# Attention products with the values issued directly behind the next step's transposes, instead of ahead of the transposes of the step after that

## Chip, cores and metric

The kernel runs on one core of a Trainium2 chip. The metric is the device time of one execution in microseconds (us), as the median of several runs. The core has a matrix engine (TensorE, PE in the profile; PEld is its weight load), a vector engine (DVE), an activation engine (ACT), GpSimd (POOL) and a queue that issues DMAs (SP). Each engine works through its own instructions in program order and waits at semaphores for the others.

## What is computed

One layer of a hybrid attention trunk for 1024 prompt frames and 64 sample frames, model width 1024. Two branches of 8 heads of 64 each: "sb" (stick-breaking attention over all earlier keys) and "cb" (softmax attention over a band of 640 keys with a relative bias). All is in float32. The part that the change touches is the attention itself:

```python
z = jnp.einsum("bqhd,bkhd->bhqk", q, k).astype(jnp.float32) * ATTN_SCALE
...
w = jnp.where(causal, jnp.exp(log_beta + suffix), 0.0)          # sb
return jnp.einsum("bhqk,bkhd->bqhd", w.astype(v.dtype), v)
...
p = jax.nn.softmax(s, axis=-1).astype(v.dtype)                  # cb
return jnp.einsum("...hqk,...khd->...qhd", p, v)
```

Before it stands one large input projection, and behind it the two gated branch projections and the output projection.

## The kernel before

The kernel is one program with an order written out by hand: each engine's instructions stand in the order in which the Python code emits them. About the first 547 us are the normalisation and the input projection (`L467`, `L673`). From 547 us to about 826 us the attention runs, and the last 145 us are the merge and the output projection (`L990`, `L1507`).

**The attention loop.** It goes through `seq`, a list of 136 steps: for each branch (sb, then cb) 4 pairs of heads, and for each pair 17 steps: one for the sample frames (t = 8, both heads at once), then 8 blocks of 128 prompt rows, each for head 0 and head 1. A step has four stages, which different iterations i of the loop issue:

- `qk(i)`, line 1096: the scores, PE matmuls in `F32R` of up to 512 columns into a PSUM tile `z` (three buffers; a step with more than 512 keys takes two). They are emptied by ACT for sb (the sigmoid of line 1099) and by DVE for cb (line 1101, `kp`/`sm` being its running minimum).
- `soft` and `mid`, in the next iteration or two: for sb one DVE scan over the row (line 1118), for cb an exponential on ACT (1109), a reciprocal on DVE (1120) and a scaling on ACT (1121).
- `tr(i - 4)`, line 1149: the weights `be`, 128 rows by up to 1024 keys, are transposed by PE, one 128 by 128 block an instruction, in groups of up to four into a PSUM tile `pt` (two buffers). Each group is copied out into `wT` by ACT (1158; 1154 for a block of 64 keys) or, three times in four in the cb branch, by DVE (1160). `LAG = 4` is the distance in steps.
- `av(b, p, j)`, line 1188: the product of transposed weights and values. One call serves 256 query rows, both heads: block pair j = 0 to 3, or j = 4 for the sample frames, so five calls for each pair of heads. The two heads use two halves of the PE array (64 columns each, `128*64` in the profile), while all other matmuls around use the whole array (`128*128`). The result stands in the PSUM tile `o` (one buffer); DVE multiplies it with the gate in `zt` (line 1197 in sb, 1199 in cb), and a POOL DMA stores it to `d_osb` or `d_ocb` (line 746, issued by `flush` an iteration later).

**Fills.** Matmuls of other projections are strewn between (`fill(n)`, lines 842 and 948, `acc`): one to three for a step in cb, fewer in sb. Half of an iteration's number stands ahead of the transposes, half behind.

**The queue of products.** When `tr` of the last step that a product needs has been issued, in iteration i, `avq` takes a note of it (line 1299), with the iteration i + 2 as its due time. The loop looks for due products (line 1293) just ahead of `tr`.

Of the kernel before, what the change touches and what calls it, by code (L numbers as in the profile page):

```python
# [32 lines left out]
def hybrid_step_kernel(ctx: ExitStack, tc: tile.TileContext, x_prompt, x_sample, c_sbk, c_sbv, c_cbk, c_cbv,  # L33
# [702 lines left out]
    def flush(every=False):  # L736
        todo = deferred[:]
        deferred.clear()
        for n, f in todo:
            if n <= 0 or every:  # L740
                f()
            else:
                deferred.append((n - 1, f))

    def store_later(dst, src, n=0):
        deferred.append((0, lambda: G.dma_start(dst, src)))  # L746
# [304 lines left out]
    def fill(n):  # L1051
        n += owed[0]
        owed[0] = 0
        while n > 0:
# [9 lines left out]
    seq = [(b, p, t, hd) for b in ("sb", "cb") for p in range(NPAIR) for t in [8] + list(range(8))  # L1064
           for hd in range(2) if t < 8 or hd == 0]

    def band(b, t):
        if t == 8:
            return 0, 576
        if b == "sb":  # L1070
            return 0, (t + 1) * 128
        k0 = max(0, t - 4)
        return k0, (t + 1 - k0) * 128
# [31 lines left out]
    def soft(i):  # L1105
        n = band(*seq[i][::2])[1]
        be, kp = st[i]
        j = 1 if n > 512 else 0
        A.activation(be[:, :n], be[:, :n], AF.Exp, bias=kp[:, j:j + 1], scale=-1.0, accum_out=kp[:, 2:3])  # L1109

    def mid(i):
        b, p, t, hd = seq[i]
        r = 128
        k0, n = band(b, t)
        be, kp = st[i]
        if b == "sb":
            im = ims[:] if t == 8 else imp[:, NP - n:NP]
            V.tensor_tensor_scan(be[:r, n - 1::-1], be[:r, n - 1::-1], im[:, ::-1], 0.0, op0=OP.mult, op1=OP.max)  # L1118
        else:
            V.reciprocal(kp[:r, 3:4], kp[:r, 2:3])  # L1120
            A.activation(be[:r, :n], be[:r, :n], AF.Copy, scale=kp[:r, 3:4])  # L1121

    def wbase(b, j):
        return max(0, 2 * j - 4) if b == "cb" and j < 4 else 0
# [3 lines left out]
    def tr(i):  # L1128
        b, p, t, hd = seq[i]
        r = 128  # L1130
        k0, n = band(b, t)
        be, _ = st.pop(i)
        j = t // 2 if t < 8 else 4
        q0 = (t % 2) * 128 if t < 8 else 0
        s0 = k0 - wbase(b, j)
        nblk = (n + 127) // 128
        groups = {}
        for kb in range(nblk):
            groups.setdefault((s0 + kb) // 4, []).append(kb)
        for g, kbs in groups.items():  # L1140
            wk = (b, p, j, hd, g)
            if wk not in wT:
                wT[wk] = ak.tile([128, 4, 256], F32, name="wT", bufs=6)
            w = wT[wk]
            pt = psT.tile([128, 4, 128], F32, name="pt")
            kr = 128
            for x, kb in enumerate(kbs):
                kr = min(128, n - kb * 128)
                TE.transpose(pt[:kr, x, :r], be[:r, kb * 128:kb * 128 + kr], ident[:r, :r])  # L1149
            m = len(kbs)  # L1150
            sl = (s0 + kbs[0]) % 4
            if kr < 128:
                m -= 1
                A.activation(w[:kr, sl + m, q0:q0 + r], pt[:kr, m, :r], AF.Copy)
            if m:
                flip[0] += 1
                if b == "sb" or flip[0] % 4 == 0:
                    A.activation(w[:, sl:sl + m, q0:q0 + r], pt[:, :m, :r], AF.Copy)  # L1158
                else:
                    V.tensor_copy(w[:, sl:sl + m, q0:q0 + r], pt[:, :m, :r])  # L1160


    def load_z(b, p, j):
        zt = ak.tile([128, 256], F32, name="zt", bufs=4)
        nq = 256 if j < 4 else 64
        SP.dma_start(zt[:, :nq], d_z[b][p][:, 256 * j:256 * j + nq])
        zts[b, p, j] = zt

    def av(b, p, j):
        o = psO.tile([128, 256], F32, name="o")  # L1170
        vp, vs = VP[b, p]
        if j == 4:
            nq = 64
            steps = [(kb, 0, 64) for kb in range(5)]
        else:
            nq = 256
            lo = 2 * j - 3 if b == "cb" else 0
            steps = [(kb, 0, 256) for kb in range(max(0, lo), 2 * j + 1)]
            if lo > 0:
                steps.append((lo - 1, 0, 128))  # L1180
            steps.append((2 * j + 1, 128, 256))
        base = wbase(b, j)
        for si, (kb, c0, c1) in enumerate(steps):
            vv = vp if j < 4 else vs
            kr = 64 if j == 4 and kb == 4 else 128
            s = kb - base
            for hd in range(2):
                TE.matmul(o[hd * 64:hd * 64 + 64, c0:c1], vv[:kr, kb, hd * 64:hd * 64 + 64],  # L1188
                          wT[b, p, j, hd, s // 4][:kr, s % 4, c0:c1] if j < 4 else
                          wT[b, p, j, 0, s // 4][:kr, s % 4, 64 * hd:64 * hd + 64],  # L1190
                          start=si == 0, stop=si == len(steps) - 1)
        os = zts.pop((b, p, j))
        if b == "sb":
            for x in range(0, nq, 128):
                y = min(x + 128, nq)
                c = 2 * j + x // 128
                V.scalar_tensor_tensor(os[:, x:y], o[:, x:y], vl[:, p, c:c + 1], os[:, x:y], op0=OP.add, op1=OP.mult)  # L1197
        else:
            V.tensor_tensor(out=os[:, :nq], in0=o[:, :nq], in1=os[:, :nq], op=OP.mult)
        o0 = 256 * (j % 3)  # L1200
        store_later(d_o[b][p][j // 3][:, o0:o0 + nq], os[:, :nq], 1)
        for k in [k for k in wT if k[:3] == (b, p, j)]:
            wT.pop(k)
# [22 lines left out]
    def load_bias(h):  # L1226
        bt = ab.tile([128, 640], F32, name="bias", bufs=4)
        src = d_rb[h][0:1, 127:128]
        SP.dma_start(bt, bass.AP(tensor=src.tensor, offset=src.offset, ap=[[767, 128], [1, 640]]))
        G.memset(bt[0:64, 576:640], BIG)  # L1230
        G.memset(bt[64:128, 0:64], BIG)
        BI[h] = bt
        if h % 2:
            bs = BI["s", h // 2] = ab.tile([128, 576], F32, name="bsm", bufs=1)
            for w in range(2):
                src = d_rb[h - 1 + w][0:1, 127:128]
                SP.dma_start(bs[64 * w:64 * w + 64], bass.AP(tensor=src.tensor, offset=src.offset,
                                                             ap=[[767, 64], [1, 576]]))
# [19 lines left out]
    LAG = 4  # L1258
    avq = []
    for i in range(len(seq) + LAG + 2):  # L1260
        m = 0
        if i < len(seq):
            b, p, t, hd = seq[i]
            if b == "cb" and p == 0 and t == 8 and hd == 0:
                sbx.close()
                yst = ExitStack()
                late["y"] = yst.enter_context(tc.tile_pool(name="ay", bufs=2))
            if (b, p, t, hd) == ("sb", 3, 6, 0):
                load_bias(0)
                load_bias(1)  # L1270
        if 0 < i <= len(seq) and seq[i - 1][0] == "cb":
            soft(i - 1)
        if 1 < i <= len(seq) + 1 and seq[i - 2][0] == "cb":
            mid(i - 2)
        if i < len(seq):
            qk(i)
            if hd == 0:
                if t % 2 == 1 or t == 8 and (b, p) != ("sb", 0):
                    load_z(b, p, t // 2 if t < 8 else 4)
                prefetch(b, p, t)  # L1280
            acc += amount[b] * wt[b](band(b, t)[1]) / tot[b]
            acc += early.get((b, p, t, hd), 0)
            m = int(acc) - emitted
            emitted += m
        else:
            m = 8
        if 0 < i <= len(seq) and seq[i - 1][0] == "sb":
            mid(i - 1)
        flush()
        if i == len(seq) // 2 + LAG + 3:  # L1290
            late["sb"] = True
        fill(m // 2)
        while avq and avq[0][0] <= i:
            av(*avq.pop(0)[1:])
        if 0 <= i - LAG < len(seq):
            tr(i - LAG)
            b, p, t, hd = seq[i - LAG]
            if t == 8 or hd == 1 and t % 2 == 1:
                avq.append((i + 2, b, p, t // 2 if t < 8 else 4))
        fill(m - m // 2)  # L1300
    flush(True)
    yst.close()
# [177 lines left out]
    for i in range(2):  # L1480
# [3 lines left out]
        for q, s in enumerate(OP_):  # L1484
# [14 lines left out]
            for c in range(2) if s != "b" else ():  # L1499
# [9 lines left out]
                p = ps[:]  # L1509
# [15 lines left out]
                if s in (3, 4, 5, 6):  # L1525
# [4 lines left out]
                    if s == 4:  # L1530
                        p, x = u3[c], xrs.pop((i, 1, 1, c))
# [61 lines left out]
```

## Time and profile before

| | us |
|---|---|
| runs of the kernel | 974.56 median of 3 (973.98 to 976.94) |
| the profiled execution, its own time | 972.79 |
| its span | 971.0 |
| of it up to the attention | 547 |
| attention | 279 |
| merge and output projection | 145 |

The profile is one execution. Its page gives busy times, the chain of work that ended last, and groups of instructions by line; other views used below are the waits (who waited for whom), the timeline (instructions in order of time, neighbours of one kind merged) and the windows (busy time of each engine in a stretch of time). In a timeline row the first number is the start, the second the length from the first start to the last end, in us. Matmuls overlap in PE's pipeline: the distance between two starts is the time that the first one costs, its own length is longer.

The TensorE clock was granted in full over the whole span after the first slice. In the attention DVE and ACT are busy most of the time too:

```profile
547.00:680.00 133.00, 130.91 (x1051) 106.85 (x1049) 102.19 (x129) 93.49 (x233) 15.77 (x32) 1.00 0.81 216
680.00:826.00 146.00, 143.12 (x1103) 125.47 (x1104) 103.61 (x373) 107.11 (x235) 31.90 (x48) 1.00 0.71 199
```

These are two windows, the sb and the cb part. The columns are: stretch, its length, then busy time and number of instructions of PE, PEld, DVE, ACT and POOL, the granted clock, the busy share of the DMA engines and GB/s.

### The profile page before, as it was taken

What the parts mean: (1) busy time and instruction counts of PE and PEld (TensorE: products, weight loads), DVE (VectorE), ACT (ScalarE), POOL (GpSimd) and SP (SyncE); (2) the same over time, 40 slices, a digit from 0 to 9 for tenths busy, and PEclk for the clock granted to TensorE, in tenths of its full rate; (3) what the DMA queues carried; (4) which work ended last, traced back from release to release, by engine and by line L of the source; (5) the groups of instructions that cost most, each with busy time, mean ns of one, the idle gap of its engine ahead of it and who ended that gap; (6) DMA issues with size and microseconds to landing.
All of it is one profiled execution on the core that took longest, in us unless ns stands there. A gap on an engine that the chain in (4) does not pass through costs nothing.

```text
span 971.0 us, 20418 instructions
## 1 busy us (share of the span) xinstructions
PE 951.1 (98%) x7604; PEld 906.3 (93%) x7604; DVE 590.2 (61%) x1166; ACT 477.4 (49%) x1056; POOL 394.5 (41%) x391
## 2 busy tenths in 40 slices
PE   5999999999999999999999999999999999999998
PEld 5999999999999999999999987787888888999998
DVE  5456665696454555543332298777678775499735
ACT  6544443344444343333332377668687775466220
POOL 3276664215454566655542200101520111586632
PEclk9999999999999999999999999999999999999999
DMA  7727567534646655555533997668699852862732
GB/s 237 224 88 246 197 219 251 182 93 133 182 139 192 183 179 175 156 177 171 165 90 101 279 252 196 186 175 241 207 278 263 226 144 75 254 203 70 222 118 92
DMA packets 173512, 176.28 MB, mean 182 GB/s; under 512 B 30753, under 2 KB 157597, under 8 KB 173286
## 3 DMA queue, kind: packets, MB, share of 16 engines
q1 hardware_dynamic: 161878, 159.98, 55.5%
q10 hardware_dynamic: 8720, 8.33, 2.7%
q0 software_dynamic: 2816, 6.69, 2.1%
q8 instruction: 60, 0.98, 0.5%
q14 instruction: 38, 0.31, 0.1%
HBM read 112.94 MB, written 62.00 MB: 180 GB/s over the span
## 4 chain that ended last, share of the span: by engine, by line
PE 92%; DMA 3%; ACT 2%; issue 1%; POOL 1%; DVE 1%; SPq 0%; ACTq 0%; POOLq 0%; DVEq 0%
PE b L673 30%; PE acc L467 20%; PE b L1507 8%; PE o L1188 7%; PE pt L1149 7%; PE z L1096 6%; PE b L990 5%; PE acc L948 4%; PE acc L842 2%; PE pk L352 1%; DMA wrawx<-in_w_in_dram 1%; DMA wraw<-in_w_in_dram 1%; DMA d_gcb<-sg 1%; PE pt L280 1%; ACT be L1109 1%
## 5 line engine op out<-in xcount | busy, mean ns | idle before, releaser
L1149 PE MATMUL pt<-ident,be 128*128 128x128 f32 (+1 forms) x568 | 87.5, 278 | 2.8 <-ACT wT L1158 1.9
L1096 PE MATMUL z<-ks,sq 128*128 128x320 f32 (+5 forms) x384 | 87.4, 336 | 1.7 <-DVE sm L1101 1.7
L1118 DVE TENSOR_TENSOR_SCAN be<-be,imp 128x128 f32<-128x128 f32 (+7 forms) x64 | 83.4, 1343 | 9.2 <-ACT be L1099 9.2
L1149 PEld LDWEIGHTS pt<-ident,be 128*128 128x128 f32 (+1 forms) x568 | 66.2, 140 | 16.2 <-issue 5.4
L1158 ACT ACTIVATE wT<-pt 128x512 f32<-128x512 f32 (+3 forms) x125 | 58.0, 496 | 41.7 <-PE pt L1149 41.2
L467 PE MATMUL acc<-whi,xa 128*128 128x256 f32 x256 | 74.2, 292 | 0.0
L467 PE MATMUL acc<-wlox,xm 128*128 128x256 f32 x256 | 70.8, 278 | 0.0
L467 PE MATMUL acc<-whi,xm 128*128 128x256 f32 x256 | 70.8, 278 | 0.0
L467 PE MATMUL acc<-wlo,xa 128*128 128x256 f32 x256 | 70.7, 278 | 0.0
L467 PE MATMUL acc<-whix,xb 128*128 128x256 f32 x256 | 70.6, 278 | 0.0
L467 PE MATMUL acc<-whix,xm 128*128 128x256 f32 x256 | 70.6, 278 | 0.0
L681 DVE TENSOR_TENSOR u<-b,s 128x256 f32<-128x256 f32 (+1 forms) x56 | 24.3, 440 | 73.5 <-PE b L673 72.4
L1096 PEld LDWEIGHTS z<-ks,sq 128*128 128x128 f32 x384 | 63.8, 190 | 3.4 <-DVE sm L1101 2.0
L1188 PE MATMUL o<-wT,vp 128*64 128x256 f32 (+1 forms) x608 | 64.2, 356 | 0.0
L1188 PEld LDWEIGHTS o<-wT,vp 128*64 128x64 f32 x608 | 40.3, 136 | 23.1 <-issue 6.2
L124 POOL TENSOR_TENSOR wlo<-wraw,whi 128x1024 fp32r<-128x1024 f32 x15 | 36.5, 2431 | 56.1 <-ACT whi L117 50.7
L1121 ACT ACTIVATE be<-be,sm 128x640 f32<-128x640 f32 (+5 forms) x68 | 47.5, 698 | 15.2 <-DVE sm L1120 14.8
L746 POOL DMA_DIRECT2D d_osb<-zt x20 | 10.8, 542 | 102.5 <-DVE zt L1197 63.9
L1099 ACT ACTIVATE be<-z 128x384 f32<-128x384 f32 (+6 forms) x104 | 47.8, 512 | 4.8 <-PE z L1096 4.1
L437 POOL TENSOR_TENSOR whix<-ws,whix 128x512 fp32r<-128x512 f32 x28 | 37.1, 1324 | 32.0 <-ACT whix L436 32.0
L1109 ACT ACTIVATE be<-be,sm 128x640 f32<-128x640 f32 (+5 forms) x68 | 47.5, 699 | 3.1 <-DVE sm L1101 2.5
L467 PEld LDWEIGHTS acc<-whi,xa 128*128 128x128 f32 x256 | 47.9, 188 | 0.1
(306 smaller groups left out, 3187.8 us busy)
## 6 DMA issues: line engine op xcount, KB each, us to landing
wraw<-in_w_in_dram SPq DMA_DIRECT2D x31, 512.0 KB, 4.5
wrawx<-in_w_in_dram SPq DMA_DIRECT2D x17, 512.0 KB, 4.2
sq<-d_qsbT SPq DMA_DIRECT2D x32, 192.0 KB, 4.8
sq<-d_qcbT SPq DMA_DIRECT2D x32, 192.0 KB, 5.2
xt<-in_x_prompt_dram SPq DMA_DIRECT2D x8, 512.0 KB, 5.4
d_kcbT<-hl SPq DMA_DIRECT2D x8, 512.0 KB, 4.3
d_qcbT<-hl SPq DMA_DIRECT2D x8, 512.0 KB, 3.1
d_ksbT<-hl SPq DMA_DIRECT2D x16, 256.0 KB, 2.9
```

The source lines that it names most:

```text
L467: TE.matmul(ps, x, w, start=m == 0, stop=m == len(steps) - 1)
L673: TE.matmul(ps[:, :m], w[:, hl_, k], right[s](x)[:, k, a:b], start=s < 3 and k == 0 and e == 0, stop=k == 3 and e == 2, skip_group_check=s ...
L990: TE.matmul(pp[uu][:, :n], w[:, p, uu * 128:uu * 128 + 128], g[:, a:e], start=p == 0 and m == 0, stop=p == NPAIR - 1 and m == 2)
L1096: TE.matmul(z[:, :m], s[:, e, q0:q0 + 128], ks[:, h, o + x:o + y], start=(e, h) == parts[0], stop=(e, h) == parts[-1])
L1099: A.activation(be[:r, x:y], z[:r, :m], AF.Sigmoid, scale=-0.125)
L1109: A.activation(be[:, :n], be[:, :n], AF.Exp, bias=kp[:, j:j + 1], scale=-1.0, accum_out=kp[:, 2:3])
L1118: V.tensor_tensor_scan(be[:r, n - 1::-1], be[:r, n - 1::-1], im[:, ::-1], 0.0, op0=OP.mult, op1=OP.max)
L1121: A.activation(be[:r, :n], be[:r, :n], AF.Copy, scale=kp[:r, 3:4])
L1149: TE.transpose(pt[:kr, x, :r], be[:r, kb * 128:kb * 128 + kr], ident[:r, :r])
L1158: A.activation(w[:, sl:sl + m, q0:q0 + r], pt[:, :m, :r], AF.Copy)
L1188: TE.matmul(o[hd * 64:hd * 64 + 64, c0:c1], vv[:kr, kb, hd * 64:hd * 64 + 64], wT[b, p, j, hd, s // 4][:kr, s % 4, c0:c1] if j < 4 else wT ...
L1507: TE.matmul(ps[:, t], left[s](xs_, k)[:, ts_], wt_[:, k], start=s < 3 and t == k == e == 0, stop=k == 3 and e == 2, skip_group_check=s > 2 ...
```

## The change

A product is no longer due two iterations after its last transposes, ahead of that iteration's transposes. It is issued in the next iteration, directly behind that iteration's transposes and ahead of the second half of its fills.

```diff
         fill(m // 2)
-        while avq and avq[0][0] <= i:
-            av(*avq.pop(0)[1:])
         if 0 <= i - LAG < len(seq):
             tr(i - LAG)
+        for todo in avq:
+            av(*todo)
+        avq.clear()
+        if 0 <= i - LAG < len(seq):
             b, p, t, hd = seq[i - LAG]
             if t == 8 or hd == 1 and t % 2 == 1:
-                avq.append((i + 2, b, p, t // 2 if t < 8 else 4))
+                avq.append((b, p, t // 2 if t < 8 else 4))
         fill(m - m // 2)
```

So each of the 40 products moves, in program order, ahead of the second half of one iteration's fills, one `qk`, and the first half of the next iteration's fills. It stays between the same two groups of transposes.

On PE in the sb part, where there is no fill at this place: `o` is the product, `z` the scores, `pt` the transposes.

```order
 L1149 MATMUL pt<-ident,be 128x128 x5
-L1096 MATMUL z<-ks,sq_7420 128x448 x4
 L1188 MATMUL o<-wT,vp 64x256 x6
 L1188 MATMUL o<-wT,vp 64x128 x2
+L1096 MATMUL z<-ks,sq_7420 128x448 x4
 L1149 MATMUL pt<-ident,be 128x128 x5
```

The scores of the following step have gone from ahead of the product to behind it. What stood directly behind the product were transposes, and is now a score matmul.

On PE in the cb part, at the end of a pair of heads, where `acc` are the fills:

```order
 L1149 MATMUL pt<-ident,be 128x128 x5
-L948 MATMUL acc<-xa,whi 128x384
-L948 MATMUL acc<-xb,whi 128x384
-L1096 MATMUL z<-ks,sq_10015 128x128 x2
-L948 MATMUL acc<-xa,wlo 128x384
 L1188 MATMUL o<-wT,vp 64x256 x8
 L1188 MATMUL o<-wT,vp 64x128 x4
+L948 MATMUL acc<-xa,whi 128x384
+L948 MATMUL acc<-xb,whi 128x384
+L1096 MATMUL z<-ks,sq_10015 128x128 x2
+L948 MATMUL acc<-xa,wlo 128x384
 L1149 MATMUL pt<-ident,be 128x128 x5
```

Three fills and the scores have changed sides. The product is entered from transposes now, and left into a fill.

On DVE at such a place in the cb part, first before, then with the change. `zt` is the multiplication that empties the product, `be,sm` empties the scores, `wT` are copies of transposes:

```order
L1120 RECIPROCAL sm<-sm 128x1
L1101 ISA be,sm<-z,bias 128x128
L1101 ISA sm 128x1
L1199 TENSOR_TENSOR zt<-o,zt 128x256
L1160 COPY wT<-pt 128x4x128
L1160 COPY wT<-pt 128x128
```

```order
L1160 COPY wT<-pt 128x4x128
L1199 TENSOR_TENSOR zt<-o,zt 128x256
L1120 RECIPROCAL sm<-sm 128x1
L1101 ISA be,sm<-z,bias 128x128
L1101 ISA sm 128x1
L1160 COPY wT<-pt 128x4x128
L1160 COPY wT<-pt 128x128
```

The multiplication has moved from directly ahead of the copies of one group of transposes to ahead of the reciprocal and the emptying of the scores. On ACT and SP nothing changes its order; on POOL a few stores of products change places with a split of a weight block (line 124) or of a gated output (line 909).

## The prediction

> **What bounds the kernel now.** I read the page first, then the waits of PE within the attention (547 to 826 us), then PE's timeline at single products, and last DVE's and ACT's rows there.
>
> ```profile
> PE 951.1 (98%) x7604; PEld 906.3 (93%) x7604; DVE 590.2 (61%) x1166; ACT 477.4 (49%) x1056; POOL 394.5 (41%) x391
> PE 92%; DMA 3%; ACT 2%; issue 1%; POOL 1%; DVE 1%; SPq 0%; ACTq 0%; POOLq 0%; DVEq 0%
> ```
>
> PE is busy for 98% of the span, and 92% of the chain that ended last is PE's. So the time is the sum of PE's work and the change can act in two ways only: by what PE pays at the seams between kinds of matmuls, and by waits that it makes or removes. The waits in the attention are few:
>
> ```profile
> PE pt L1149 <- ACT wT L1158: 1.9, 5, 0.6
> PE z L1096 <- DVE sm L1101: 1.7, 1, 1.7
> PE pt L1149 <- DVE wT L1160: 0.7, 2, 0.4
> PE o L1188 <- PE z L1096: 0.3, 2, 0.2
> ```
>
> Columns: us in total, times, longest. In all 4.6 us of 279: that is the most that better order alone could take away. No product waits for its copies in `wT`, though it is the product that would be drawn nearer to them.
>
> **The change part by part.** It adds and removes no instruction. It moves 40 products, one for each store:
>
> ```profile
> L746 POOL DMA_DIRECT2D d_ocb<-zt x20 | 10.9, 547 | 72.2 <-DVE zt L1199 39.4 <-DVE sm L1120 17.7 <-DMA gt<-d_gsb 8.5
> L746 POOL DMA_DIRECT2D d_osb<-zt x20 | 10.8, 542 | 102.5 <-DVE zt L1197 63.9 <-DVE be L1118 16.2 <-DVE sm L1120 8.1
> ```
>
> First the seams. Products use half the array's columns for each head, all else the whole array. Two places show what entering and leaving a product costs. The last product of all stands between fills, the only such place before:
>
> ```profile
> 821.87 0.34 PE L948 MATMUL acc<-xa,wlo 128*128 128x384 f32 x1
> 822.04 0.34 PE L948 MATMUL acc<-xa,whi 128*128 128x384 f32 x1
> 822.31 2.38 PE L1188 MATMUL o<-wT,vp 128*64 128x256 f32 x24
> 824.62 0.44 PE L948 MATMUL acc<-xb,whi 128*128 128x384 f32 x1
> 824.90 0.33 PE L948 MATMUL acc<-xa,wlo 128*128 128x384 f32 x1
> 825.08 0.34 PE L948 MATMUL acc<-xa,whi 128*128 128x384 f32 x1
> ```
>
> A fill of 384 columns costs 0.17 to 0.18 us from start to start. The one ahead of the product costs 0.27: **entering** is 0.10. From the product's start to the next matmul's are 2.31 us. The first fill behind it is 0.44 long where others are 0.34, and the next starts 0.28 later instead of 0.17: **leaving into a fill** adds 0.105. Now the usual place, a product of the same 24 matmuls left into a transpose, and five transposes behind a product and not behind one:
>
> ```profile
> 753.80 2.38 PE L1188 MATMUL o<-wT,vp 128*64 128x256 f32 x24
> 756.11 0.33 PE L1149 MATMUL pt<-ident,be 128*128 128x128 f32 x1
> ...
> 815.59 0.76 PE L1149 MATMUL pt<-ident,be 128*128 128x128 f32 x5
> 816.11 0.42 PE L948 MATMUL acc<-xa,wlo 128*128 128x384 f32 x1
> 816.37 0.30 PE L948 MATMUL acc<-xa,whi 128*128 128x320 f32 x1
> ...
> 817.24 0.31 PE L948 MATMUL acc<-xa,whi 128*128 128x320 f32 x1
> 817.39 0.71 PE L1149 MATMUL pt<-ident,be 128*128 128x128 f32 x5
> 817.86 0.40 PE L948 MATMUL acc<-xb,whi 128*128 128x320 f32 x1
> 818.09 0.31 PE L948 MATMUL acc<-xa,wlo 128*128 128x320 f32 x1
> ```
>
> The product again takes 2.31. **Leaving into transposes** adds 0.05 (0.52 against 0.47 for five). A fill goes into transposes at no charge (0.15 for 320 columns, as between fills). A fill behind transposes shows 0.26 instead of 0.175 because it starts early, in the transposes' tail: five transposes truly cost 0.47 + 0.085 = 0.555.
>
> The last row of this kind needed, transposes into a product, is in no trace of before. Nearest are transposes that use 64 of the array's rows and are followed by a whole-array transpose or a fill:
>
> ```profile
> 59.47 0.34 PE L352 MATMUL pk<-ident,qn 64*128 64x64 f32 x2
> 59.73 0.66 PE L374 MATMUL pc<-ident,ck 128*128 128x128 f32 x4
> ...
> 87.14 0.34 PE L352 MATMUL pk<-ident,qn 64*128 64x64 f32 x2
> 87.40 0.39 PE L467 MATMUL acc<-whi,xa 128*128 128x256 f32 x1
> 87.63 0.28 PE L467 MATMUL acc<-whi,xm 128*128 128x256 f32 x1
> 87.75 0.28 PE L467 MATMUL acc<-wlo,xa 128*128 128x256 f32 x1
> ```
>
> Two transposes of 64 columns need half of two of 128, 2 x 0.055 = 0.11, and the second half of the price of leaving them: from 59.47 to 59.73 are 0.26, 0.15 over it. Of that 0.05 is what the first transpose behind a changed array costs (as above), so 0.10 is the emptying of the array, as much as a fill pays. It is the same whether a transpose or a fill follows (87.14 to 87.40). I therefore take 0.10 for transposes into a product. The last two rows give the price of leaving into a fill again: 0.23 against 0.12.
>
> The sum for one product, over the same matmuls, in starts (fill F, product P, five transposes T): before, F to P 0.27, P 2.31, T 0.52, F 0.26, together 3.36. After, F to T 0.175, T to P 0.555 + 0.10, P 2.31, F 0.28, together 3.42. That is **0.06 us more for each product**, all of it because the first matmul behind a product is now a fill or a score matmul (both load 128 columns in `F32R`) and waits longer for its weights than a transpose did. 40 x 0.06 = **+2.4 us**; with rounding of rows to 0.01 it may be 1.6 to 2.8, and I use +2.2. Bounds where the row is lacking: if T to P is free, 40 x (0.06 - 0.10) = -1.6; if it also pays 0.05 for the first weights, 40 x 0.11 = +4.4.
>
> The profile's two weight loads say where the 0.05 comes from:
>
> ```profile
> L1149 PEld LDWEIGHTS pt<-ident,be 128*128 128x128 f32 (+1 forms) x568 | 66.2, 140 | 16.2 <-issue 5.4
> L1096 PEld LDWEIGHTS z<-ks,sq 128*128 128x128 f32 x384 | 63.8, 190 | 3.4 <-DVE sm L1101 2.0
> ```
>
> A transpose's load lasts 140 ns, a score matmul's 190, a difference of 0.05. The Trainium skill says otherwise: by "TensorE: Matmul & The Clock Gate", section "LDWEIGHTS (loading the stationary operand)", a load depends on the number of columns alone, here 128 for both. By it leaving would cost the same either way, and the seams would sum to zero instead of +2.2. The rows speak against it, and I go by them.
>
> Next the waits. A product now stands only one step behind its last transposes. What hides the copies into `wT` is that iteration's scores, fills and transposes; with two groups the next transposes need the same `pt` buffers and so wait for these copies already. The tightest place is the first product of an sb pair, with single groups:
>
> ```profile
> 621.19 0.40 ACT L1158 ACTIVATE wT<-pt 128x256 f32<-128x256 f32 x1
> 621.24 0.49 PE L1149 MATMUL pt<-ident,be 128*128 128x128 f32 x3
> 621.45 0.80 ACT L1099 ACTIVATE be<-z 128x320 f32<-128x320 f32 x2
> ```
>
> The copy (first row) ends at 621.59, the three transposes' work at about 621.24 + 0.33 = 621.57: no wait, but no room. Were it 0.2 late at the 4 places, it cost 0.8. On DVE, the queue behind the multiplication of `zt` waits for the product's end, before as after; what is queued there changes from copies of transposes to a reciprocal and the emptying of the scores that now follow the product. At the ends of cb pairs this helps:
>
> ```profile
> 748.62 0.42 DVE L1199 TENSOR_TENSOR zt<-o,zt 128x256 f32<-128x256 f32 x1 [1.70 <-PE o L1188]
> 749.20 0.89 DVE L1160 COPY wT<-pt 128x512 f32<-128x512 f32 x2 [0.15 <-PE pt L1149]
> 749.94 0.77 PE L1149 MATMUL pt<-ident,be 128*128 128x128 f32 x5 [0.33 <-DVE wT L1160]
> ```
>
> Here copies queue behind the multiplication, and the next transposes wait. With the change the multiplication is done earlier: perhaps 0.3 at three places, -0.9. Against it, the scores' emptying in the middle of cb pairs, formerly done under the product, follows it now. I set the waits at zero, between -4.6 (all that there are) and what the first rival below costs. The one large wait, 1.69 us at 694.62, is a score matmul behind DVE, and the product that stood behind it moves ahead of it:
>
> ```profile
> 694.62 0.56 PE L1096 MATMUL z<-ks,sq 128*128 128x320 f32 x2 [1.69 <-DVE sm L1101]
> 695.40 0.87 PE L1188 MATMUL o<-wT,vp 128*64 128x256 f32 x8
> ```
>
> It can hide up to 0.87 of that wait, but DVE, late there, makes the following scores wait instead: zero again. Stores are issued one iteration earlier in the same queue; a weight split on POOL that now stands behind one more store is many fills ahead of its use. SP's order stays.
>
> Sum: 972.79 + 2.2 = 975.0 for an execution like the profiled one, which lay 1.8 under the median of its kernel's runs. In terms of that median: 974.56 + 2.2 = **976.8**.
>
> **Rivals.** *A, ACT or DVE become the bound between products (slower).* In sb, ACT used to empty the scores ahead of a product under it; now it does only the last copies under it. That moves two sigmoids into the stretch between products (the row at 621.45, 0.80 us for two) and one step's copies out of it (about 0.5): +0.3 for each of 16 long stretches in sb, 4.8 us, decided where ACT has no slack: 93.49 of 133 us busy speaks against it over the whole, the waits of transposes on ACT (1.9) for it at the ends of pairs. With the seams 974.56 + 2.2 + 4.8 = 981.6; a third of it would do for "slower". *B, the waits for copies go.* The rows at 748.62 speak for it. All 1.9 + 0.7 gone: 974.56 + 2.2 - 2.6 = 974.2. *C, transposes into a product need no emptying and no wait for weights*, since both are plain float32: 40 x (0.06 - 0.15) = -3.6, 971.0. The pair at 59.47 speaks against it. So does the Trainium skill, "TensorEngine Tiling (Array Packing)", section "Key Properties": a change of tiling mode drains the engine. By that rule, the trace agrees (0.10 at each change seen).
>
> **How the numbers follow.** Forecast 0.50, A 0.28, B 0.14, C 0.08. A measurement of this kernel tells about 0.3% (2.9 us) from no change, so "same" reaches from 971.6 to 977.5. The forecast, 976.8 give or take 1, is same in four cases of five (0.40) and slower in one (0.10); A is slower but for 0.02; B is same; C is faster. Slower 0.36, same 0.56, faster 0.08. The range leaves out C and the upper half of A's cases: 973.0 to 981.0; the forecast's own is 975.5 to 978.
>
> **What would show it.** In the timeline after: the first matmul behind each product about 0.1 longer than its like; 0.65 from five transposes to a product; the sb window longer by about 1.1 us and the cb window by as much, PE's waits within a microsecond of 4.6. Rival A would show as waits of transposes or scores on ACT or DVE above 7 us, B as these waits gone, C as less than 0.60 from five transposes to a product. The prediction is wrong if PE's waits in the attention change by over 2 us, or if anything outside 547 to 826 us moves.

## The result and the profile after

| | before | after |
|---|---|---|
| median of 20 runs each, us | 974.55 (972.58 to 976.94) | 978.50 (976.44 to 980.66) |
| ratio, 95% interval | 1 | 1.0040 (1.0032 to 1.0047) |
| profiled execution, its own time, us | 972.79 | 980.66 |
| from the first score matmul to the first of the branch projection (`L990`), us | 287.95 | 294.18 |
| from there to the end of PE's work, us | 130.95 | 130.95 |

The kernel became 0.40% slower, 3.95 us in the medians, where 2.2 us were forecast. The profiled execution of after is the slowest of its 20 and shows a difference of 7.9 us: 1.6 of it lies ahead of the attention, in code that is the same, and 6.2 between the two marks in the table. Only these 6.2 us are explained here.

The page's busy times, of the kernel after:

```profile
PE 957.4 (98%) x7604; PEld 913.4 (93%) x7604; DVE 591.5 (60%) x1166; ACT 476.4 (49%) x1056; POOL 392.8 (40%) x391
```

PE is the bound as before. Its busy time has grown by 6.3 us with the same 7604 matmuls, so not all of the loss is waiting. The waits of PE (us in total, times, longest), after:

```profile
PE acc L948 <- DVE xm L952: 2.9, 1, 2.9
...
PE pt L1149 <- ACT wT L1158: 1.6, 4, 0.6
PE o L1188 <- ACT wT L1158: 1.1, 1, 1.1
PE pt L1149 <- DVE wT L1160: 0.7, 2, 0.4
PE z L1096 <- DVE sm L1101: 0.6, 1, 0.6
```

The last four are the attention's: 4.0 us where 4.6 were. The first one is new in size (0.2 before): PE waits for a free PSUM buffer `acc`. It stands behind the attention, in the fills of the gate. First the seams (the passages from one kind of matmul to another), in PE's timeline after, at a cb product:

```profile
720.54 0.34 PE L948 MATMUL acc<-xb,whi 128*128 128x384 f32 x1
720.72 0.74 PE L1149 MATMUL pt<-ident,be 128*128 128x128 f32 x5
721.38 2.38 PE L1188 MATMUL o<-wT,vp 128*64 128x256 f32 x24
723.70 0.44 PE L948 MATMUL acc<-xa,wlo 128*128 128x384 f32 x1
723.98 0.52 PE L1096 MATMUL z<-ks,sq 128*128 128x384 f32 x2
```

In starts: fill to transposes 0.18, five transposes to the product 0.66, the product 2.32, the fill behind it 0.28. Now the end of the attention in the same view, with the last product and the one large wait:

```profile
824.28 0.31 PE L948 MATMUL acc<-xb,whi 128*128 128x320 f32 x1
824.52 2.38 PE L1188 MATMUL o<-wT,vp 128*64 128x256 f32 x24
826.83 0.41 PE L948 MATMUL acc<-xa,wlo 128*128 128x320 f32 x1
...
835.39 0.34 PE L948 MATMUL acc<-xa,wlo 128*128 128x384 f32 x1
838.59 0.41 PE L948 MATMUL acc<-xa,whi 128*128 128x320 f32 x1 [2.86 <-DVE xm L952]
...
839.01 0.47 PE L948 MATMUL acc<-xa,wlo 128*128 128x320 f32 x1
...
842.21 0.38 PE L948 MATMUL acc<-xa,wlo 128*128 128x320 f32 x1
842.43 0.31 PE L948 MATMUL acc<-xa,whi 128*128 128x320 f32 x1
842.57 0.31 PE L948 MATMUL acc<-xb,whi 128*128 128x320 f32 x1
```

In the kernel after, 835.39 to 838.59 are 3.20 us, a stall of 2.65 us more than before, where the same two fills are 0.55 apart:

```profile
831.71 0.34 PE L948 MATMUL acc<-xa,wlo 128*128 128x384 f32 x1
832.26 0.42 PE L948 MATMUL acc<-xa,whi 128*128 128x320 f32 x1 [0.21 <-DVE xm L952]
```

Behind the stall twelve fills, 839.01 to 842.21, follow each other in 0.267 us, where the last rows show 0.147: 1.44 us more. The windows of after (length, then busy time and instructions of PE, PEld, DVE, ACT and POOL, the granted clock, DMA share, GB/s) say why:

```profile
834.00:838.00 4.00, 1.73 (x10) 1.40 (x8) 2.25 (x3) 1.87 (x4) 2.27 (x2) 1.00 0.50 171
838.00:842.00 4.00, 3.41 (x14) 3.41 (x15) 1.08 (x4) 1.82 (x4) 2.08 (x3) 0.62 0.87 278
```

The granted clock falls to 0.62 in the window behind the stall. So of 6.2 us, 4.1 are in this one place.

What is late there is read from DVE's timeline. First before, then after:

```profile
821.19 0.49 DVE L952 TENSOR_TENSOR xm<-acc,gt 128x320 f32<-128x320 f32 x1 [0.98 <-PE acc L948]
824.74 0.42 DVE L1199 TENSOR_TENSOR zt<-o,zt 128x256 f32<-128x256 f32 x1 [3.06 <-PE o L1188]
...
829.50 0.77 DVE L909 TENSOR_TENSOR og<-ot,og 128x384 fp32r<-128x384 f32 x1 [1.05 <-ACT og L904]
...
831.66 1.01 DVE L952 TENSOR_TENSOR xm<-acc,gt 128x384 f32<-128x384 f32 x2
```

```profile
826.95 0.42 DVE L1199 TENSOR_TENSOR zt<-o,zt 128x256 f32<-128x256 f32 x1 [3.16 <-PE o L1188]
827.29 0.48 DVE L952 TENSOR_TENSOR xm<-acc,gt 128x320 f32<-128x320 f32 x1
...
835.75 2.31 DVE L909 TENSOR_TENSOR og<-ot,og 128x384 fp32r<-128x384 f32 x2 [3.67 <-ACT og L904]
837.99 1.01 DVE L952 TENSOR_TENSOR xm<-acc,gt 128x384 f32<-128x384 f32 x2
```

Before, a group of fills ended ahead of the last product: its emptying (`L952`) was done at 821.68, and the multiplication `L1199` came 3 us later. After, the last product stands between the eleventh and the twelfth fill of that group. The group ends 2.3 us later (the product), and its emptying comes behind the multiplication. SP's next gate load (`gt`) waits for that emptying, which frees its buffer. Such waits are a row of their own in the queue's waits of the kernel after (before: 17.6 us in 5 waits, so the dependence is old; the row does not show its lateness):

```profile
SPq L923 <- DVE xm L952: 16.5, 3, 10.3
```

SP's timeline, before and after:

```profile
821.71 0.80 SPq L923 DMA_DIRECT2D gt<-d_gsb  x2
822.62 1.45 SPq L886 DMA_DIRECT2D wraw<-in_w_proj_cb_dram  x2
824.11 2.15 SPq L899 DMA_DIRECT2D ot<-d_ocb  x4
```

```profile
827.80 0.80 SPq L923 DMA_DIRECT2D gt<-d_gsb  x2
828.70 1.10 SPq L886 DMA_DIRECT2D wraw<-in_w_proj_cb_dram  x2
829.84 2.18 SPq L899 DMA_DIRECT2D ot<-d_ocb  x4
```

In both the gate load starts 0.03 us behind the end of the emptying (821.68 and 827.77). Behind the gate load stand a load of projection weights and the loads of the cb outputs (`ot`), 5.7 us later than before on the clock of the trace, of which some 3.6 are the later start (1.6) and the seams (about 2, below). ACT's and DVE's splitting of these outputs (`L904`, `L909`) follow, and on DVE the emptying of the next two groups of fills (`L952`, 831.66 before, 837.99 after) is queued behind `L909`. PE has no free `acc` until then.

### The profile page after: what moved, and what is told of

It is laid out like the page before. It is cut to its first block, busy times and chain, and to the rows that moved or that the text cites. A ratio compares the mean times of both kernels' runs of the same rounds, so it can differ in the third digit from the quotient of the medians.

```text
span 978.9 us, 20413 instructions
## 1 busy us (share of the span) xinstructions
PE 957.4 (98%) x7604; PEld 913.4 (93%) x7604; DVE 591.5 (60%) x1166; ACT 476.4 (49%) x1056; POOL 392.8 (40%) x391
## 4 chain that ended last, share of the span: by engine, by line
PE 93%; DMA 2%; ACT 2%; issue 1%; POOL 1%; DVE 0%; SPq 0%; DVEq 0%; ACTq 0%; POOLq 0%
PE b L673 30%; PE acc L467 20%; PE b L1509 8%; PE o L1188 7%; PE z L1096 7%; PE pt L1149 6%; PE b L990 5%; PE acc L948 5%; PE acc L842 4%; PE pk L352 1%; DMA wrawx<-in_w_in_dram 1%; PE pt L280 1%; PE acc L1545 1%; DMA gt<-d_gsb 0%; DMA d_gcb<-sg 0%
```

## The experiments

The ratios below are to runs of the kernel before made beside each experiment (medians 974.35 us for the first four, 974.22 for the others), and each has its 95% interval; "the marks" are the two of the table above.

Theory T: two separate costs. The seams cost 1.5 to 2 us over all products, and the last product alone costs the rest, by the stall at the end of the attention and the slow clock behind it. Rival R: the cost is spread over the attention, with products too close behind their copies into `wT`.

**The last product at its old place, the 39 others at their new one** (change to the kernel after):

```diff
-        for todo in avq:
-            av(*todo)
-        avq.clear()
+        if i != len(seq) + LAG:
+            for todo in avq:
+                av(*todo)
+            avq.clear()
```

> The changed kernel, with the last product alone (the 40th, between fills) back at its old place, half an iteration of fills later. Theory T (the seams cost +2.0 us over 39 products, the rest is the stall of fills at 838.6 us that the last product's move brings about: its multiplication stands ahead of an emptying of a fill on DVE, which lets the next gate load go, and with it the loads of the cb outputs): the stall falls from 3.1 us back to about 0.5, no slow clock behind it, time 976.5 (ratio to before 1.002). Rival R (the whole +3.9 is spread over the attention, the stall is one execution's accident): stall and time as in the changed kernel, 978.5 (1.004).

Measured: 975.86 us (12 runs, 975.08 to 979.88), ratio 1.0013 (1.0002 to 1.0024). The distance between the marks is 290.55. PE's timeline at the tail (the end of the attention):

```profile
835.80 0.42 PE L948 MATMUL acc<-xa,whi 128*128 128x320 f32 x1 [1.00 <-DVE xm L952]
836.06 0.31 PE L948 MATMUL acc<-xb,whi 128*128 128x320 f32 x1
```

A wait of 1.0 us is left, and the fills behind it go on at the full clock, 0.31 long.

**The last product alone moved** (change to the kernel before):

```diff
-                avq.append((i + 2, b, p, t // 2 if t < 8 else 4))
+                avq.append((i + (2 if i - LAG < len(seq) - 1 else 1), b, p, t // 2 if t < 8 else 4))
```

> The kernel before, with the last product alone moved to its new place; all other 39 stay. Theory T: the stall comes, 2.6 us more than before, and up to 1.9 us of slow clock behind it where the clock drops: 976.7 to 978 (ratio 1.002 to 1.004). Rival R: no change, 974.6 (1.000), the one seam that differs is worth 0.06 us.

Measured: 977.77 us (975.18 to 979.09), ratio 1.0026 (1.0017 to 1.0036). One product of 40 brings the whole stall; PE's timeline, and the window behind it:

```profile
835.71 0.41 PE L948 MATMUL acc<-xa,whi 128*128 128x320 f32 x1 [2.73 <-DVE xm L952]
```

```profile
835.00:839.00 4.00, 3.29 (x14) 3.29 (x15) 1.33 (x4) 1.78 (x4) 2.17 (x3) 0.67 0.83 262
```

The two parts add up, 0.13% and 0.26% against 0.40% for the whole, within intervals of about 0.1% either way. By the medians they are 1.5 and 3.4 us against 3.95. Not all of the second is the last product's: in the profiled execution the clock fell a second time, at 696 us, behind a wait that the kernel before has too (last section). Rival R would have left nearly all of the loss to the 39.

**One fill ahead of the last product** (change to the kernel after): the group of fills is complete before the product, and nothing else moves.

```diff
+        if i == len(seq) + LAG:
+            fill(1)
+            m -= 2
         for todo in avq:
             av(*todo)
```

> The changed kernel, with one fill (the twelfth and last of its group) issued ahead of the last product instead of behind it; nothing else moves. Theory T: that fill completes a group, whose emptying then stands ahead of the product's multiplication on DVE; the gate load and the loads behind it go some 2.5 us earlier, the stall falls to under 1 us, time 976.5 (1.002). If the stall hangs on when the last product is computed or stored rather than on this order, it stays: 978.5 (1.004).

Measured: 975.55 us (973.74 to 977.11), ratio 1.0007 (0.9997 to 1.0017). DVE's timeline shows the emptying ahead of the multiplication again; the wait at the tail is 1.0 us, as in the first experiment:

```profile
824.25 0.49 DVE L952 TENSOR_TENSOR xm<-acc,gt 128x320 f32<-128x320 f32 x1 [0.99 <-PE acc L948]
826.58 0.42 DVE L1199 TENSOR_TENSOR zt<-o,zt 128x256 f32<-128x256 f32 x1 [1.83 <-PE o L1188]
```

All 40 products are at their new place here. One matmul ahead of one product takes back about three quarters of the loss (978.50 to 975.55).

**Products ahead of the last group of the next step's transposes,** where that step has several groups, so that a product is left into transposes as before (24 products); where it has one group, the old place (16 products). Change to the kernel after, its core:

```diff
...
-        for g, kbs in groups.items():
+        for n_, (g, kbs) in enumerate(groups.items()):
+            if n_ and n_ == len(groups) - 1:
+                for todo in between:
+                    av(*todo)
...
+        return len(groups) > 1
...
-        if 0 <= i - LAG < len(seq):
-            tr(i - LAG)
-        for todo in avq:
+        for todo in late_av:
             av(*todo)
+        late_av.clear()
+        todo = avq[:]
         avq.clear()
         if 0 <= i - LAG < len(seq):
+            if not tr(i - LAG, todo):
+                late_av.extend(todo)
...
```

> Products stand in the same iteration as in the changed kernel, but ahead of the last group of that iteration's transposes where there are two groups (24 of 40), so that a product is left into transposes as before; the other 16, the last among them, keep their old place. Theory T (the cost is leaving into a fill or score matmul, 0.06 us each, and the last product): seams as before, time 974.6 within 0.5 (ratio 1.000), give or take waits for the last copies, which the product now follows more closely, up to 0.3 us at each of 24 (7 us, visible as waits of products on ACT or DVE). Rival R (standing one step earlier costs by itself, ACT and DVE being bound): 24 of 40 of the cost, 976.9 (1.0024), with waits of transposes and scores.

Measured: 976.18 us (974.89 to 978.92), ratio 1.0016 (1.0007 to 1.0026). The seams went as expected: PE's time between the marks without its idle time is 282.98 us, where it is 282.77 before and 284.88 in the first experiment, in which 39 products stand as in the kernel after. But PE got a new wait at the passage from sb to cb. Its waits, and ACT's timeline there:

```profile
PE pt L1152 <- ACT wT L1161: 3.3, 4, 1.9
```

```profile
670.29 1.28 ACT L1109 ACT_TABLE_LOAD   x1
671.59 0.78 ACT L1109 ACTIVATE be<-be,sm 128x576 f32<-128x576 f32 x1
...
672.36 0.95 ACT L1161 ACTIVATE wT<-pt 128x512 f32<-128x512 f32 x2
```

The copy is queued behind the change of the activation table and an exponential, and the transposes that need its buffer have no product ahead of them to cover it. Between the marks are 290.15 us, 2.2 more than before. At this place the last score matmul and the first transpose start 2.22 us apart, 0.52 before, and at the tail the two fills 1.36 apart, 0.55 before. These two together are 2.5 us, a little over the 2.2 by which the marks moved: no dearer seams, no other loss. The time itself missed what was expected, by the wait at the passage and the one at the tail.

**`og_lo` (the low part of the split of a cb output, `L909`) of the first cb block wholly on POOL,** in the kernel after and in the one before, so that on DVE no emptying of fills is queued behind `L909`. In both:

```diff
-        (V if p % 2 and (b, ci) != ("cb", 1) else G).tensor_tensor(
+        (V if p % 2 and (b, ci) not in (("cb", 0), ("cb", 1)) else G).tensor_tensor(
```

> The changed kernel, with the odd second products of the first og_lo tile of the cb block computed on POOL instead of DVE, so that the emptying of the gate's scores and the last fills' emptying on DVE are queued behind nothing that waits for the late output load. Theory T (the stall at the tail is a queue effect: the last multiplication stands ahead of an emptying on DVE, SP's gate load and output load follow late, and DVE's og_lo piece holds the next emptying): PE's wait on the emptying of acc at the tail, 2.9 us in the changed kernel, is under 0.5, no stretch of fills at half rate follows, and the time is 975.5 to 976.3, 1.0010 to 1.0018 of before; what is left is the seams. Rival (the late loads themselves hold the end, whichever engine computes og_lo): the same 2 to 3 us come back as a wait of the last projection on ACT or POOL, 977.5 to 978.8.

Measured: 977.31 us (975.11 to 979.58), ratio 1.0029 (1.0018 to 1.0040). The stall among the fills is gone, and 289.46 us lie between the marks, 1.5 over before: the seams alone. But from the second mark to the end there are 135.38 us in place of 130.95. PE's timeline in the branch projection:

```profile
850.70 0.61 PE L990 MATMUL b<-og,whi 128*128 128x384 f32 x2 [0.49 <-ACT whi L117]
851.96 0.44 PE L990 MATMUL b<-og,wlo 128*128 128x384 f32 x1 [0.65 <-DVE wlo L124]
```

Counted from the first score matmul, PE came to the projection 4.7 us sooner than in the kernel after (289.46 for 294.18), but SP issued the cb loads no sooner (280.2 us behind that mark, 280.3 in the kernel after), and PE waits for weights there. The largest of these waits stands in PE's waits:

```profile
PE b L990 <- POOL wlo L124: 1.8, 1, 1.8
```

Both sides were half right: DVE's queue made that stall, and the rival was right that the loss comes back in the last projection. How much of these 4.4 us is the lateness of the loads and how much the longer work of POOL is not separated: SP's second group of cb loads comes 288.1 us behind the first mark where it is 287.3 in the kernel after, and the kernel before with the same edit, below, loses only 0.25 there. What takes it away is the edit of the third experiment, which gives SP its buffer sooner.

> The kernel before with the same piece of og_lo on POOL. Theory T: its own small wait at that place (0.5 to 1.3 us with what follows) goes too, 973.3 to 974.3, 0.9987 to 0.9998 of before. Rival: POOL becomes late with og_lo for the last projection and the wait moves there, 974.5 to 976.

Measured: 974.29 us (972.39 to 977.99), ratio 1.0001 (0.9989 to 1.0013). Between the marks 0.4 us are gained, behind them 0.25 are lost. There is nothing to be had at this place in the kernel before. No kernel here was faster than it.

**The old distance with the new order.** Each product comes two iterations later as before, but behind that iteration's transposes (change to the kernel before):

```diff
-        while avq and avq[0][0] <= i:
-            av(*avq.pop(0)[1:])
         if 0 <= i - LAG < len(seq):
             tr(i - LAG)
+        while avq and avq[0][0] <= i:
+            av(*avq.pop(0)[1:])
+        if 0 <= i - LAG < len(seq):
             b, p, t, hd = seq[i - LAG]
```

> Order without nearness: as before each product comes two steps after its last transposes, but behind the transposes of that step, not ahead of them; the last product has no transposes beside it and stays where it was. Theory T: the seams are paid by the order alone (39 times 0.04 to 0.06 us, +1.6 to +2.3, PE's waits in the attention aside), the stall at the tail is as before (about 1 us with what follows it), 975.6 to 976.9, 1.0010 to 1.0024. Rival (the cost of the changed kernel beside its tail comes from standing close behind the copies, not from the seams): no more than 0.5 us over before, 974.0 to 975.0.

Measured: 978.99 us (6 runs, 978.16 to 979.49), ratio 1.0046 (1.0032 to 1.0060). Both expectations missed. The tail has 0.6 us of wait, and the seams are those of the kernel after (the first matmul behind a product 0.107 us dearer, as there), so they are indeed paid by the order alone. But between the marks are 293.49 us, 5.5 more than before, and the seams account for about 2. PE waits for copies of transposes 5.0 us in 11 places, where it is 2.6 in 7; counted in starts, gaps of over 0.15 us sum to 2.5 us more than before. The last microsecond lies in smaller gaps and was not assigned. PE's waits, and its timeline at one place; then the same place before:

```profile
PE pt L1149 <- ACT wT L1158: 3.7, 8, 1.5
```

```profile
645.75 0.33 PE L1149 MATMUL pt<-ident,be 128*128 128x128 f32 x1 [0.21 <-ACT wT L1158]
646.01 3.46 PE L1188 MATMUL o<-wT,vp 128*64 128x256 f32 x32
```

```profile
644.34 3.46 PE L1188 MATMUL o<-wT,vp 128*64 128x256 f32 x32
647.73 0.33 PE L1149 MATMUL pt<-ident,be 128*128 128x128 f32 x1
```

The long product used to stand between the two groups of transposes and covered the copies that free `pt`. Here it has gone past the second group, which waits. In the change itself the product stays between the same two groups and only passes scores and fills. That is why its waits hardly changed; I had not seen in the prediction that this was the reason.

## Why the prediction was right and wrong

- **What bounds the kernel:** right, PE before and after.
- **The seams:** right in kind and in size. At the place shown, 0.66 for five transposes to a product was 0.655 in the forecast, and 0.28 for the fill behind a product was 0.28; the unknown price of transposes into a product, taken as 0.10, held. At all 40 places the first matmul behind a product takes, from its start to the next, 0.107 us more than the same matmul among its like; before, at the 24 places where several transposes followed, it was 0.056. PE's time between the marks without its idle time, 282.77 us before, is 284.88, 284.77 and 284.68 in the first, third and fifth experiments, in whose profiles the clock did not fall there: +1.9 to +2.1, about 0.05 for a product, where 0.06 and +2.2 were used. In the fifth, with 0.4 us less of idle time, the marks are 1.5 us further apart. The old-distance kernel shows that the order pays the seams.
- **A product is left at a lower price into transposes than into fills or scores:** shown by 0.056 against 0.107, and by the kernel with products ahead of a group of transposes, 282.98 us. That the length of the weight loads is the reason was argued from their rows and not tried.
- **The two rules weighed there:** by the Trainium skill, "TensorE: Matmul & The Clock Gate", section "LDWEIGHTS (loading the stationary operand)", the seams would have summed to zero; the runs have about +2, so the measurement decides against that sum here. By the Trainium skill, "TensorEngine Tiling (Array Packing)", section "Key Properties", a change of tiling mode drains the engine; the trace of after agrees at the new seam too (0.66 for five transposes that cost 0.555 by themselves).
- **Waits at zero within the attention:** right in the sum, 4.0 us for 4.6, within the microsecond that was given. They moved: the one of 1.69 us fell to 0.6, and 1.1 appeared ahead of the first cb product, which was said to hide "up to 0.87" of it, "zero again".
- **Rivals A, B and C:** none occurred. No product between transposes and scores made ACT or DVE the bound, the waits for copies of transposes stayed (2.3 us for 2.6), and transposes into a product were not free.
- **The step that failed** is the one on the queues. It named what is queued behind the multiplication on DVE for the middle and the end of pairs only, and closed SP with "SP's order stays". SP's order did stay, but its instructions wait: the last product moved ahead of the last fill of a group, the group's emptying came later, and SP's gate load with all loads behind it became late with that emptying. This costs 0.27% of the time, 2.6 us (ratio 1.0040 with, 1.0013 without the last product's move). The prediction had the place in its quoted rows (the last product between fills, at 822.31) and used it for a price only. Its own mark for being wrong, anything that moves outside 547 to 826 us, is the one that was met.
- **The sum:** 2.2 forecast; measured, by the ratios, 1.3 for 39 products and 2.5 for the last one, 3.95 in all. The range of 973.0 to 981.0 held 978.50, but by luck: its upper part was laid out for rival A, which did not occur. The forecast's own range, to 978, was missed by 0.5 us, and what went over it is the tail, for which the sum had no term. "Same" was the likeliest case and, by the prediction's own bound of 0.3%, "slower" came true, with 0.1% over it.

## What to carry to other kernels

A moved block must be followed at the two ends of its loop too, not at its usual places alone: there the neighbours are others, and a single matmul that ends a group late can hold a buffer, a load queue and everything queued behind it. Where an in-order queue stays in order, ask what each of its entries waits for, since one late release shifts all that follow. And a block that covers a copy may pass other work freely, but not the instructions that wait for that copy.

## What the hardware showed

A single gap in PE's work can be followed by a stretch at half clock, and the price of it comes on top of the gap. In the kernel after the granted clock is 0.50 from 838.95 to 842.36 us, behind 2.86 us of idling, and fills of 320 columns took 0.267 us there in place of 0.147. In the kernel with only the last product moved there are two such stretches, each 3.41 us long: one behind the stall of 2.73 us, and one, at 696.42, behind a wait of 1.76 us for DVE that the change does not touch. The same wait before, 1.69 us at 694.62, and the one of 1.94 us in the fourth experiment were not followed by one, nor were those of 1.0 us at the tail.

So the length of the gap alone does not decide it. In all nine profiles every change of the granted clock lies a whole number of steps of 3.413 us behind the first grant of the full clock, the fall in the kernel after at 241 steps (822.61 us). Laid over the waits, this grid has the 2.86, 2.73 and 1.76 us each inside one of its steps. The 1.69 us is divided by a step's edge into 0.70 and 0.99, the 1.94 us into 1.48 and 0.46. In these profiles a wait with 1.76 us or more inside one step brought the slow stretch, three times of three, and waits with 1.52 us or less inside one did not; no experiment was made on it. Where the edges fall differs between executions, and so does the clock: one slow stretch makes a mean clock of 0.998 here, and 14 of the 20 runs of the kernel after have that, with a median of 978.8, while the other six have 1.0 and 977.1. Of the runs of before beside the experiments 20 of 58 have 0.998 or less, of the second, fourth and sixth experiments, which keep that wait for DVE, 22 of 36, and of the other four, whose longest wait between the marks is 1.5 us, 1 of 42.

The Trainium skill, "TensorE: Matmul & The Clock Gate", section "Part 1: The HAM clock gate (the "warmup" mystery)", puts the array at half rate after an idle window of about 3.4 us, with a window that runs freely. Half rate, the length of the slow stretch and the fixed grid agree with the traces here. The threshold doesn't: 1.76 us of waiting in one step were enough here.
